# A decoder layer's feed-forward part as seven block products on token halves, and linear attention in 64-column tiles

## The chip, the cores and the metric

One core of a Trainium2 chip runs the whole layer in one launch. The metric is device time in microseconds (us), the median of several runs. In the profile PE is TensorE (PEld its weight loads), DVE is VectorE, ACT is ScalarE, POOL is GpSimd and SP is the queue that issues nearly all DMAs. L200 is line 200 of the kernel.

## The reference

One layer works on 1024 prompt tokens and 8 x 8 sample tokens, 1088 in all, with 1024 features. Everything is float32.

```python
xn = rmsnorm(x, g_mix); proj = xn @ w_in            # linear attention (4 heads) and softmax heads (8)
o_g = rmsnorm(gla(...)) * silu(r)
h = x + concat(o_g, o_s) @ w_out
hn = rmsnorm(h, g_ffn)
y = rmsnorm(h + (silu(hn @ w_fg) * (hn @ w_fu)) @ w_fd, g_final)
```

`w_fg` and `w_fu` are 1024 x 2816, `w_fd` is 2816 x 1024. Linear attention goes in chunks with a state S of 64 x 128 for each head.

## The kernel before

Features lie on the 128 partitions, tokens along the columns, in chunks of 384, 384 and 320 (`CHUNKS`, L32). To keep float32 accuracy at the rate of the `fp32r` type each operand is split in two (`split`, L170): ScalarE rounds it to `hi`, VectorE computes `lo = raw - hi`. A product is then three (`mm3`, L196): hi x hi, hi x lo, lo x hi, added up in PSUM.

The order of the stages: input projection with linear attention in between (`gla_heads`, L537), softmax attention with projections filled in, the first half of the output projection, its second half (L1011 to L1032), feed-forward, final norm.

The second half of the output projection makes the residual `h` for each feature block and chunk and at once `hhi` and `hlo`, the split of `h` times `g_ffn`. The row norm is not in them: `rstd_bc` is multiplied in behind the products.

Feed-forward: there are 22 blocks f of 128 inner features. `ff_up(f)` (L1054) loads and splits the block of the gate and of the up weights, and for each chunk does 8 x 3 products into one PSUM bank for gate and 8 x 3 for up; VectorE multiplies each by `rstd_bc` (L1066, L1068), ScalarE does Silu (L1067), GpSimd gate times up (L1069), and the result is split (L1070). `ff_down` (L1082) takes two blocks at a time and adds 8 x 2 x 3 products for each chunk to `h` (L1090). Every weight is loaded and split once.

The order on each engine comes from the framework's planner, which follows program order, priorities (`tc.high_priority` for weights) and its own idea of durations; each engine then runs its list in that order and waits at the head. DMAs are issued by SP in the same way.

In linear attention each 128-token step (L660) multiplies, for two heads i, the 128-wide `AT` block with the values (L665) and the 128-wide `qE` block with the state (L668), each head into its own bank; copies, squares and the state update follow.

Of the kernel before, what the change touches and what calls it, by code (L numbers as in the profile page):

```python
# [36 lines left out]
BIG = 5  # L37
FILL_AT = (156, 199, 242, 273, 306)
# [64 lines left out]
def hymba_layer(  # L103
# [433 lines left out]
    def gla_heads(g, q, k, V, Vs):  # L537
# [33 lines left out]
        for part in range(3):  # L571
# [86 lines left out]
            if part < 2:  # L658
                otok = gla.tile([P, 8, P], F32, tag="otok", name="otok", bufs=2)
                for c in range(ncmb):  # L660
                    tt = part * 4 + c
                    for i in range(2):
                        o = bank("AX"[i])[:, :P]
                        hs = slice(64 * i, 64 * i + 64)
                        mm(out=o, lhsT=AT[:, i * ncmb + c, :], rhs=V[part][:, c, i * P : (i + 1) * P],  # L665
                           start=True, stop=S is None)
                        if S is not None:
                            mm(out=o, lhsT=qE[hs, c * P : c * P + P], rhs=S[hs, :], start=False, stop=True)  # L668
                        x = 2 * c + i
                        vec.tensor_copy(out=otok[:, x, :], in_=o)  # L670
                        square_sum(o, ssg[:, x : x + 1])
# [331 lines left out]
    late = open_pool("late", side="left")  # L1003
    h = late.tile([P, KT, TT], F32, name="h")
    ff = open_pool("hn", side="right")
    hhi = ff.tile([P, KT, TT], F32R, name="hhi")
    hlo = ff.tile([P, KT, TT], F32R, name="hlo")
    outp = open_pool("outp", side="left")
    ones = outp.tile([P, 1], F32, name="ones")
    vec.memset(ones, 1.0)  # L1010
    os = [load_o(outp, c, 1) for c in range(3)]  # L1011
    sq_acc = [outp.tile([P, 384], F32, tag="acc", name="acc", bufs=3) for _ in CHUNKS]
    for f in range(KT):
        if f % 2 == 0:
            ws = load_w_out(f, 1)
        for c, (c0, n) in enumerate(CHUNKS):
            cs = slice(c0, c0 + n)
            xa = outp.tile([P, 384], F32, tag="xa", name="xa", bufs=4)[:, :n]
            dma(out=xa, in_=x_dram[:, f, cs])
            ps = bank("mm")  # L1020
            mm3(ps[:, :n], ws[f % 2], os[c])
            vec.tensor_tensor(out=h[:, f, cs], in0=ps[:, :n], in1=xa, op=ALU.add)

            act(out=hhi[:, f, cs], in_=h[:, f, cs], func=AF.Copy, scale=gf[:, f : f + 1])
            vec.scalar_tensor_tensor(out=hlo[:, f, cs], in0=h[:, f, cs], scalar=gf[:, f : f + 1],
                                     in1=hhi[:, f, cs].bitcast(F32), op0=ALU.mult, op1=ALU.subtract)
            if f == 0:
                act(out=sq_acc[c][:, :n], in_=h[:, f, cs], func=AF.Square)
            else:
                sq = outp.tile([P, 384], F32, tag="sq", name="sq", bufs=2)  # L1030
                act(out=sq[:, :n], in_=h[:, f, cs], func=AF.Square)
                pool.tensor_tensor(out=sq_acc[c][:, :n], in0=sq_acc[c][:, :n], in1=sq[:, :n], op=ALU.add)  # L1032
    st = outp.tile([P, 3, NTT + 1], F32, name="st")
    vec.memset(st, 1.0)
    tiles = [(c, j, 3 * c + j, min(P, n - j * P)) for c, (_, n) in enumerate(CHUNKS) for j in range(-(-n // P))]
    ps = bank("A")
    for c, j, t, m in tiles:
        mm(out=ps[:m, t : t + 1], lhsT=sq_acc[c][:, j * P : j * P + m], rhs=ones, start=True, stop=True)
    vec.tensor_copy(out=st[:, 0, :NTT], in_=ps[:, :NTT])
    vec.tensor_copy(out=st[:TS, 0, NTT:], in_=ps[:TS, NTT : NTT + 1])  # L1040
    rms(st[:, 1, :], st[:, 0, :], D, st[:, 2, :])
    rows = outp.tile([P, NTT + 1, P], F32, name="rows")
    vec.tensor_copy(out=rows, in_=st[:, 1, :].unsqueeze(2).broadcast_to([P, NTT + 1, P]))
    rb = [bank(tag)[:, :n] for tag, (_, n) in zip("ATT", CHUNKS)]
    for c, j, t, m in tiles:
        nc.tensor.transpose(out=rb[c][:, j * P : j * P + m], in_=rows[:m, t, :], identity=ident[:m, :m])
    for c, (c0, n) in enumerate(CHUNKS):
        vec.tensor_copy(out=rstd_bc[:, c0 : c0 + n], in_=rb[c])
    outp.release()


    ffp = open_pool("ffn", side="left")

    def ff_up(f):  # L1054
        wg_, wu_ = load_w(w_fg[:, f * P : (f + 1) * P]), load_w(w_fu[:, f * P : (f + 1) * P], room=(ffp, "wuraw"))
        ghi = ffp.tile([P, TT], F32R, tag="ghi", name="ghi", bufs=4)
        glo = ffp.tile([P, TT], F32R, tag="glo", name="glo", bufs=4)
        for c0, n in CHUNKS:
            cs = slice(c0, c0 + n)
            xv = ([hhi[:, k, cs] for k in range(KT)], [hlo[:, k, cs] for k in range(KT)])  # L1060
            pg, pu = bank("mm"), bank("S")
# [8 lines left out]
            split(ghi[:, cs], glo[:, cs], gt)  # L1070
        return ghi, glo

    def load_down(f):
        with tc.high_priority():
            raw = wpool.tile([P, D], F32, tag="wraw", name="wd_raw", bufs=1)
            dma(out=raw, in_=w_fd[f * P : (f + 1) * P, :])
# [130 lines left out]
```

## Time and profile before

| what | us |
|---|---|
| median of 3 runs (1580.24 to 1588.89) | 1586.47 |
| the profiled execution | 1588.28 |
| its span in the profile | 1586.4 |
| TensorE busy | 1522.2 |
| VectorE busy | 717.3 |
| ScalarE busy | 435.6 |
| GpSimd busy | 272.1 |

The busy time of TensorE is that of matmuls in flight: they are pipelined, so the rate of products is read from the distance of their starts, not from their lengths. An idle stretch has a releaser, the event that ended it. The granted clock is a share of full speed (1.00 is 2.4 GHz).

### The profile page before, as it was taken

To read this page: it belongs to the slowest core of one execution; us is meant where nothing else is said; L and a number is where in the kernel's file an instruction comes from. 1 tells how busy PE (TensorE), PEld (TensorE's weight loads), DVE (VectorE), ACT (ScalarE), POOL (GpSimd) and SP (SyncE) were. 2 spreads that over 40 slices of the span, in tenths; PEclk is the share of its full clock that TensorE was granted. 3 is DMA by queue.
4 is the path that set the end of the run, shared out by engine and by line. 5 is a ranking of instruction groups with operands and counts; after the bars stand their busy time and mean duration, and the time that the engine had idled before them with its cause. 6 is when DMAs were issued, how large, how long until landed. Compare 5 with 4: busy or idle time off the path is not lost.

```text
span 1586.4 us, 28631 instructions
## 1 busy us (share of the span) xinstructions
PE 1522.2 (96%) x12080; PEld 1377.2 (87%) x12080; DVE 717.3 (45%) x1556; ACT 435.6 (27%) x867; POOL 272.1 (17%) x296
## 2 busy tenths in 40 slices
PE   7979999999999998997999999999999999999997
PEld 6768877887776765767999999999999999999997
DVE  5486575543323233335643443433443343444437
ACT  4143242144342445314421212121111212121113
POOL 1494342042112010002310001010000001010002
PEclk9988999999999999989999999999999999999998
DMA  5320121163443547545321101110211101120102
GB/s 155 92 78 30 30 69 43 41 188 106 136 112 93 153 118 217 177 138 175 92 74 50 54 27 54 41 54 27 67 40 41 54 27 54 40 63 18 54 1 114
DMA packets 177425, 126.73 MB, mean 80 GB/s; under 512 B 14576, under 2 KB 169104, under 8 KB 177296
## 3 DMA queue, kind: packets, MB, share of 16 engines
q1 hardware_dynamic: 173088, 124.69, 26.4%
q8 instruction: 95, 1.56, 0.4%
q10 hardware_dynamic: 4208, 0.21, 0.2%
q14 instruction: 34, 0.28, 0.1%
HBM read 101.40 MB, written 23.46 MB: 79 GB/s over the span
## 4 chain that ended last, share of the span: by engine, by line
PE 86%; DMA 5%; DVE 5%; POOL 1%; issue 1%; ACT 1%; SPq 0%; DVEq 0%; ACTq 0%; POOLq 0%
PE ps_mm L200 13%; PE ps_mm L201 12%; PE ps_mm L202 12%; PE ps_S L202 5%; PE ps_S L201 5%; PE ps_S L200 5%; PE ps_T L201 2%; PE ps_T L200 2%; PE ps_T L202 2%; PE ps_S L835 2%; DMA oraw<-o_dram 2%; PE ps_T L933 2%; PE ps_X L977 2%; PE ps_A L202 1%; PE ps_A L200 1%; PE ps_A L201 1%
## 5 line engine op out<-in xcount | busy, mean ns | idle before, releaser
L200 PE MATMUL ps_mm<-xhi,whi 128*128 128x384 f32 (+1 forms) x576 | 199.5, 347 | 2.0 <-ACT whi L171 1.6
L202 PE MATMUL ps_mm<-xhi,wlo 128*128 128x384 f32 (+1 forms) x576 | 194.6, 339 | 1.1 <-DVE wlo L172 1.1
L201 PE MATMUL ps_mm<-xlo,whi 128*128 128x384 f32 (+1 forms) x576 | 194.8, 339 | 0.2 <-DVE xlo L277 0.2
L1069 POOL TENSOR_TENSOR gt<-gt,ut 128x384 f32<-128x384 f32 (+1 forms) x66 | 64.9, 984 | 698.1 <-DVE ut L1068 698.1
L200 PE MATMUL ps_mm<-hhi,whi 128*128 128x384 f32 (+1 forms) x528 | 172.8, 327 | 1.2 <-DVE gt L1066 1.2
L202 PE MATMUL ps_mm<-hhi,wlo 128*128 128x384 f32 (+1 forms) x528 | 173.0, 328 | 0.0
L201 PE MATMUL ps_mm<-hlo,whi 128*128 128x384 f32 (+1 forms) x528 | 172.8, 327 | 0.0
L200 PE MATMUL ps_S<-hhi,whi 128*128 128x384 f32 (+1 forms) x528 | 172.7, 327 | 0.0
L201 PE MATMUL ps_S<-hlo,whi 128*128 128x384 f32 (+1 forms) x528 | 172.7, 327 | 0.0
L202 PE MATMUL ps_S<-hhi,wlo 128*128 128x384 f32 (+1 forms) x528 | 172.5, 327 | 0.0
L200 PEld LDWEIGHTS ps_mm<-xhi,whi 128*128 128x128 f32 x576 | 110.2, 192 | 13.6 <-issue 7.6
L202 PEld LDWEIGHTS ps_mm<-xhi,wlo 128*128 128x128 f32 x576 | 110.2, 191 | 7.3 <-issue 4.8
L201 PEld LDWEIGHTS ps_mm<-xlo,whi 128*128 128x128 f32 x576 | 110.4, 192 | 5.5 <-issue 4.0
L1067 ACT ACTIVATE gt<-gt 128x384 f32<-128x384 f32 (+1 forms) x66 | 33.1, 502 | 294.6 <-DVE gt L1066 294.6
L1068 DVE TENSOR_TENSOR ut<-ps_S,rstd_bc 128x384 f32<-128x384 f32 (+1 forms) x66 | 35.4, 536 | 159.7 <-PE ps_S L202 159.7
L200 PEld LDWEIGHTS ps_mm<-hhi,whi 128*128 128x128 f32 x528 | 99.2, 188 | 1.4 <-DVE gt L1066 1.4
L201 PEld LDWEIGHTS ps_S<-hlo,whi 128*128 128x128 f32 x528 | 99.2, 188 | 0.0
L202 PEld LDWEIGHTS ps_mm<-hhi,wlo 128*128 128x128 f32 x528 | 99.2, 188 | 0.0
L202 PEld LDWEIGHTS ps_S<-hhi,wlo 128*128 128x128 f32 x528 | 99.2, 188 | 0.0
L200 PEld LDWEIGHTS ps_S<-hhi,whi 128*128 128x128 f32 x528 | 99.2, 188 | 0.0
L201 PEld LDWEIGHTS ps_mm<-hlo,whi 128*128 128x128 f32 x528 | 99.2, 188 | 0.0
L1090 DVE TENSOR_TENSOR h<-h,ps_T 128x384 f32<-128x384 f32 (+1 forms) x120 | 63.5, 529 | 68.1 <-PE ps_T L202 68.1
(335 smaller groups left out, 3048.4 us busy)
## 6 DMA issues: line engine op xcount, KB each, us to landing
wraw<-in_w_in_dram SPq DMA_DIRECT2D x22, 512.0 KB, 3.8
wraw<-in_w_ffn_gate_dram SPq DMA_DIRECT2D x22, 512.0 KB, 3.7
wd_raw<-in_w_ffn_down_dram SPq DMA_DIRECT2D x22, 512.0 KB, 3.2
wuraw<-in_w_ffn_up_dram SPq DMA_DIRECT2D x22, 512.0 KB, 3.7
raw<-in_cache_swa_k_dram SPq DMA_DIRECT2D x32, 256.0 KB, 5.4
raw<-in_cache_swa_v_dram SPq DMA_DIRECT2D x32, 256.0 KB, 4.4
xa<-x_dram SPq DMA_DIRECT2D x32, 192.0 KB, 2.6
xr<-in_x_prompt_dram SPq DMA_DIRECT2D x8, 512.0 KB, 8.4
```

What stands on the lines that cost most here:

```text
L200: mm(out=ps, lhsT=whi[k], rhs=xhi[k], start=first and k == 0, stop=False)
L201: mm(out=ps, lhsT=whi[k], rhs=xlo[k], start=False, stop=False)
L202: mm(out=ps, lhsT=wlo[k], rhs=xhi[k], start=False, stop=last and k == n - 1)
L835: ins = mm(out=out, lhsT=qres[own, qi * P + 32 * r : qi * P + 32 * r + 32], rhs=rhs, start=True, stop=True)
L933: nc.tensor.transpose(out=ps[:, r * P : (r + 1) * P], in_=raw[:, r, :], identity=ident)
L977: mm(out=av[rs, b2 * P : (b2 + 1) * P], lhsT=pT[:, t, rs], rhs=vts[b2][:, r, :], start=False, stop=t == 5 and b2 == 1)
L1067: act(out=gt, in_=gt, func=AF.Silu)
L1068: vec.tensor_tensor(out=ut, in0=pu[:, :n], in1=rstd_bc[:, cs], op=ALU.mult)
L1069: pool.tensor_tensor(out=gt, in0=gt, in1=ut, op=ALU.mult)
L1090: vec.tensor_tensor(out=h[:, k, cs], in0=h[:, k, cs], in1=ps[:, :n], op=ALU.add)
```

## The change

The tokens are cut into two halves of 2 x 272 (`NH = 272`). Weights are seen as 2 x 2 blocks A11, A12, A21, A22 (of output features by input features), activations as B of 2 x 2 (input features by tokens). Instead of eight block products there are seven, M1 to M7, in the Winograd form of Strassen's algorithm: four sums of weight blocks (S1 to S4) and four of activation blocks replace the eighth, and the seven results are combined with more additions.

`winograd` loads four weight blocks, GpSimd makes S1 to S4 in place, each of the seven blocks is split on its own, and every product is 2 x nk x 3 matmuls of 272 columns into a pair of banks. M7, M2, M3 and M4 go on in the bank pair of M6, M1, M5 and M7. `gate_up(i, xs)` does this for two gate and two up blocks (1024 columns a weight block, nk = 4), eleven times for each half of the tokens; `down(i, gs, h)` for two such i at a time (512 columns, nk = 2) in two parts q. So all feed-forward weights are loaded twice. `operand` makes the seven activation operands: four subtractions of 272 columns on GpSimd and splits of 3 x 272 and 4 x 272 columns.

The norm now goes in ahead of the products (`norm_half`), so `hhi` and `hlo` of the old kind are gone. The second half of the output projection is done per half of the tokens (`out_half`, 272 columns); half 1 of the residual goes to DRAM and is read back. The very last feed-forward block of half 1 is multiplied in the ordinary way, in chunks of 224 and 320 columns, with the final norm as before behind the last. In linear attention both products are cut into 64-column halves of the tokens.

```diff
-                    tt = part * 4 + c
+                    halves = (slice(0, 64), slice(64, 128))
+                    os_ = [bank("AX"[i])[:, :P] for i in range(2)]
                     for i in range(2):
-                        o = bank("AX"[i])[:, :P]
-                        hs = slice(64 * i, 64 * i + 64)
-                        mm(out=o, lhsT=AT[:, i * ncmb + c, :], rhs=V[part][:, c, i * P : (i + 1) * P],
-                           start=True, stop=S is None)
-                        if S is not None:
-                            mm(out=o, lhsT=qE[hs, c * P : c * P + P], rhs=S[hs, :], start=False, stop=True)
+                        for ts in halves:
+                            mm(out=os_[i][ts], lhsT=AT[:, i * ncmb + c, ts], rhs=V[part][:, c, i * P : (i + 1) * P],
+                               start=True, stop=S is None)
+                    for ts in halves if S is not None else ():
+                        for i, hs in enumerate(halves):
+                            mm(out=os_[i][ts], lhsT=qE[hs, c * P + ts.start : c * P + ts.stop], rhs=S[hs, :], start=False, stop=True)
+                    for i, o in enumerate(os_):
                         x = 2 * c + i
                         vec.tensor_copy(out=otok[:, x, :], in_=o)
                         square_sum(o, ssg[:, x : x + 1])
...
+    ORDER = (("M1", "A11", 0, "a", True), ("M6", "S2", 4, "b", True), ("M5", "S1", 3, "c", True), ("M7", "S3", 5, "b", False),
+             ("M2", "A12", 1, "a", False), ("M3", "S4", 2, "c", False), ("M4", "A22", 6, "b", False))
+    def blocks(src, w):
...
+        for name, m, k in (("A11", 0, 0), ("A21", 1, 0), ("A22", 1, 1), ("A12", 0, 1)):
+            src(room(name), m, k)
+        add = lambda out, a, b, op: pool.tensor_tensor(out=out, in0=raw[a], in1=raw[b], op=op)
+        add(room("S1"), "A21", "A22", ALU.add)
+        add(raw["A21"], "A11", "A21", ALU.subtract)
+        raw["S3"] = raw["A21"]
+        def parts(name):
+            if name == "S2":
+                add(raw["A11"], "S1", "A11", ALU.subtract)
+                raw["S2"] = raw["A11"]
+            if name == "S4":
+                add(raw["A12"], "A12", "S2", ALU.subtract)
+                raw["S4"] = raw["A12"]
...
+            split(*pair, raw[name])
+            return pair
+        return parts
+    def winograd(src, w, view, x, nk, after):
+        with tc.high_priority():
+            parts = blocks(src, w)
+        banks = {"a": psum2.tile([P, 2, 512], F32, tag="a", name="ps_a", bufs=1)[:, :, :NH]}
+        for name, block, slot, bk, first in ORDER:
+            with tc.high_priority():
+                hi, lo = (view(part) for part in parts(block))
+            if bk not in banks:
+                banks[bk] = psum2.tile([P, 2, 512], F32, tag=bk, name=f"ps_{bk}", bufs=2 if bk == "b" else 1)[:, :, :NH]
+            for s in range(2):
+                for k in range(nk):
+                    xhi, xlo = x(k, slot)
+                    one = lambda l, r, i: mm(out=banks[bk][:, s], lhsT=l[:, k, s], rhs=r, start=first and k == 0 and i == 0,
+                                             stop=k == nk - 1 and i == 2, skip_group_check=not first)
+                    one(hi, xhi, 0)
+                    one(hi, xlo, 1)
+                    one(lo, xhi, 2)
+            after(name, banks)
...
+    def operand(pl, B, tag):
+        t = ffp.tile([P, 4, NH], F32, tag="T", name="T", bufs=1)
+        sub = lambda out, a, b: pool.tensor_tensor(out=out, in0=a, in1=b, op=ALU.subtract)
+        sub(t[:, 0], B[:, 3], B[:, 0])
+        sub(t[:, 2], B[:, 2], B[:, 3])
+        sub(t[:, 1], B[:, 2], t[:, 0])
+        sub(t[:, 3], B[:, 1], t[:, 1])
+        hi, lo = (pl.tile([P, 7, NH], F32R, tag=f"{tag}{part}", name=f"{tag}{part}", bufs=4 if tag == "x" else 3) for part in ("hi", "lo"))
+        split(hi[:, 0:3], lo[:, 0:3], B[:, 0:3])
+        split(hi[:, 3:7], lo[:, 3:7], t)
+        return hi, lo
+    def norm_half(hf):
+        t0 = 2 * NH * hf
+        xs = []
+        for k in range(0, KT, 2):
+            B = new_block()
+            for j, v in ((0, B[:, 0:4:3]), (1, B[:, 1:3])):
+                if hf:
+                    dma(out=v, in_=x_dram[:, k + j, t0 : t0 + 2 * NH].rearrange("p (n t) -> p n t", t=NH))
+                vec.scalar_tensor_tensor(
+                    out=v, in0=v if hf else h[0][:, k + j].rearrange("p (n t) -> p n t", t=NH), scalar=gf[:, k + j : k + j + 1],
+                    in1=rstd_bc[:, t0 : t0 + 2 * NH].rearrange("p (n t) -> p n t", t=NH), op0=ALU.mult, op1=ALU.mult)
+            xs.append(operand(bx, B, "x"))
+        return xs
...
+    def gate_up(i, xs):
+        s1, u2, v5 = temps()
+        B = new_block()
...
+        def made(slot, c, eng):
+            act(out=B[:, slot], in_=c[:, 0], func=AF.Silu)
+            eng.tensor_tensor(out=B[:, slot], in0=B[:, slot], in1=c[:, 1], op=ALU.mult)
...
+        def after(name, ps):
+            add = lambda out, a, b: vec.tensor_tensor(out=out, in0=a, in1=ps[b], op=ALU.add)
+            if name == "M1":
+                act(out=s1, in_=ps["a"], func=AF.Copy)
+            elif name == "M6":
+                add(u2, s1, "b")
+            elif name == "M5":
+                add(v5, s1, "c")
+            elif name == "M7":
+                add(v5, v5, "b")
+                made(2, v5, pool)
+            elif name == "M2":
+                made(0, ps["a"], vec)
+            elif name == "M3":
+                add(u2, u2, "c")
+                made(3, u2, pool)
             else:
+                add(s1, s1, "b")
+                made(1, s1, pool)
+        winograd(src, KT * P, lambda t: t.rearrange("p (s k c) -> p k s c", s=2, c=P),
+                 lambda k, slot: [part[:, slot] for part in xs[k]], KT // 2, after)
+        return B
+    def down(i, gs, h):
+        n = len(gs)
+        hv = h.rearrange("p (q m) (n t) -> p q m n t", m=2, t=NH)
+        for q in range(0, KT // 2, 2):
+            s1, u2, v5 = temps()
...
+            def after(name, ps):
+                to = lambda m, n: hv[:, q : q + 2, m, n]
+                add = lambda out, a, b: vec.tensor_tensor(out=out, in0=a, in1=ps[b], op=ALU.add)
+                more = lambda out, a: pool.tensor_tensor(out=out, in0=out, in1=a, op=ALU.add)
+                if name == "M1":
+                    act(out=s1, in_=ps["a"], func=AF.Copy)
+                    more(to(1, 0), s1)
+                elif name == "M6":
+                    add(u2, s1, "b")
+                    more(to(0, 1), u2)
+                elif name == "M5":
+                    add(v5, s1, "c")
+                    more(to(1, 1), v5)
+                else:
+                    o, bk = {"M7": (to(1, 1), "b"), "M2": (to(0, 0), "a"), "M3": (to(0, 1), "c"), "M4": (to(1, 0), "b")}[name]
+                    add(o, o, bk)
+            winograd(src, n * 2 * P, lambda t: t.rearrange("p (j q c) -> p j q c", q=2, c=P),
+                     lambda k, slot: [part[:, slot] for part in gs[k]], n, after)
+    for hf in range(2):
+        out_half(hf)
+        if hf == 0:
...
+    for hf in range(2):
+        gs = {}
+        for i in range(NF // 2):
+            B = gate_up(i, xs)
+            if hf and i == NF // 2 - 1:
+                break
+            gs[i] = operand(bh, B, "g")
+            if i % 2 == 0 and i >= 2:
+                if hf == 0 and i == NF // 2 - 1:
+                    xs = norm_half(1)
+                down(i - 2, [gs[i - 2], gs[i - 1]], h[hf])
+            if hf and i == 0:
+                for t0 in range(0, 2 * NH, P):
+                    final_rows(0, t0, min(P, 2 * NH - t0))
+                h[1] = residual()
+                dma(out=h[1], in_=x_dram[:, :, 2 * NH :])
+        if hf == 0:
+            down(NF // 2 - 1, [gs[NF // 2 - 1]], h[0])
...
```

## Rows read from the trace of the kernel before

**Rows 1.** the page, part 1: busy us of each engine, share of the span, instructions
```profile
PE 1522.2 (96%) x12080; PEld 1377.2 (87%) x12080; DVE 717.3 (45%) x1556; ACT 435.6 (27%) x867; POOL 272.1 (17%) x296
```

**Rows 2.** the page, part 4: the chain that ended last, by engine
```profile
PE 86%; DMA 5%; DVE 5%; POOL 1%; issue 1%; ACT 1%; SPq 0%; DVEq 0%; ACTq 0%; POOLq 0%
```

**Rows 3.** busy time by stage: stage, length, five engines, clock, DMA share, GB/s
```profile
719.00:782.00 63.00, 55.82 (x327) 55.15 (x325) 36.46 (x61) 32.27 (x61) 23.00 (x21) 0.95 0.40 123
782.00:1560.00 778.00, 776.54 (x4721) 775.68 (x4721) 328.72 (x552) 136.40 (x210) 65.92 (x67) 1.00 0.14 44
1560.00:1587.00 27.00, 16.84 (x103) 15.60 (x101) 19.20 (x54) 10.11 (x25) 9.41 (x10) 0.82 0.43 166
```

**Rows 4.** instructions in time, TensorE, feed-forward: start, length, what (columns 384)
```profile
1008.06 0.33 PE L200 MATMUL ps_X<-ghi,wdhi 128*128 128x384 f32 x1
...
1009.97 0.33 PE L202 MATMUL ps_T<-ghi,wdlo 128*128 128x384 f32 x1
```

**Rows 5.** the same view, input projection, 320 columns
```profile
45.20 0.31 PE L200 MATMUL ps_mm<-xhi,whi 128*128 128x320 f32 x1
...
47.84 0.31 PE L200 MATMUL ps_mm<-xhi,whi 128*128 128x320 f32 x1
```

**Rows 6.** the same view, transposes at the start, four to a row
```profile
41.08 0.60 PE L266 MATMUL ps_T<-ident,xr 128*128 128x128 f32 x4
41.52 0.60 PE L266 MATMUL ps_S<-ident,xr 128*128 128x128 f32 x4
```

**Rows 7.** the same view, GpSimd, sums of 512 and 64 columns
```profile
61.98 2.54 POOL L387 TENSOR_TENSOR xt<-xhi,xlo 128x512 f32<-128x512 f32 x2
...
66.92 0.32 POOL L387 TENSOR_TENSOR xt<-xhi,xlo 128x64 f32<-128x64 f32 x1
```

**Rows 8.** groups by line, VectorE, feed-forward: count, busy us, mean ns, idle before
```profile
L172 DVE TENSOR_TENSOR wlo<-wuraw,whi 128x1024 fp32r<-128x1024 f32 x22 | 33.6, 1526 | 5.0 <-ACT whi L171 5.0
...
L172 DVE TENSOR_TENSOR wlo<-wraw,whi 128x1024 fp32r<-128x1024 f32 x21 | 25.7, 1225 | 12.1 <-ACT whi L171 12.1
L172 DVE TENSOR_TENSOR glo<-gt,ghi 128x384 fp32r<-128x384 f32 x44 | 24.6, 559 | 76.3 <-ACT ghi L171 76.3
L1068 DVE TENSOR_TENSOR ut<-ps_S,rstd_bc 128x384 f32<-128x384 f32 x44 | 24.6, 558 | 129.7 <-PE ps_S L202 129.7
```

**Rows 9.** instructions in time, GpSimd and VectorE, three places where they meet
```profile
828.99 0.88 POOL L1069 TENSOR_TENSOR gt<-gt,ut 128x320 f32<-128x320 f32 x1 [5.96 <-DVE ut L1068]
829.27 1.67 DVE L172 TENSOR_TENSOR wlo<-wuraw,whi 128x1024 fp32r<-128x1024 f32 x1 [0.46 <-ACT whi L171]
...
805.89 1.23 DVE L172 TENSOR_TENSOR wlo<-wuraw,whi 128x1024 fp32r<-128x1024 f32 x1
806.06 1.78 POOL L1069 TENSOR_TENSOR gt<-gt,ut 128x320 f32<-128x320 f32 x1 [1.72 <-DVE ut L1068]
...
854.08 0.88 POOL L1069 TENSOR_TENSOR gt<-gt,ut 128x320 f32<-128x320 f32 x1 [5.97 <-DVE ut L1068]
854.12 0.56 DVE L1090 TENSOR_TENSOR h<-h,ps_A 128x384 f32<-128x384 f32 x1 [0.22 <-PE ps_A L202]
```

**Rows 10.** groups by line, ScalarE, feed-forward
```profile
L171 ACT ACTIVATE whi<-wuraw 128x1024 fp32r<-128x1024 f32 x22 | 23.4, 1063 | 42.0 <-PE ps_S L201 42.0
```

**Rows 11.** the page, part 6: DMA issues, KB each, us to landing
```profile
wraw<-in_w_ffn_gate_dram SPq DMA_DIRECT2D x22, 512.0 KB, 3.7
```

**Rows 12.** instructions in time, TensorE, linear attention
```profile
139.93 0.49 PE L668 MATMUL ps_A<-S,qE 64*128 64x128 f32 x2
140.35 0.49 PE L665 MATMUL ps_X<-V,AT 128*128 128x128 f32 x2
```

**Rows 13.** busy time by stage around the projection's wait (columns as in rows 3)
```profile
724.00:728.00 4.00, 0.00 (x0) 0.00 (x0) 1.36 (x3) 1.03 (x2) 0.00 (x0) 0.91 0.67 237
728.00:732.00 4.00, 2.06 (x7) 2.07 (x8) 1.70 (x4) 1.55 (x4) 0.00 (x0) 0.50 0.02 6
732.00:736.00 4.00, 4.00 (x21) 4.00 (x20) 0.96 (x2) 1.03 (x2) 0.00 (x0) 0.74 0.02 3
```

More of the change, by code (lines that the diff above doesn't have):

```diff
@@ L37 @@
 BIG = 5
+NH = TT // 4
 FILL_AT = (156, 199, 242, 273, 306)
@@ L1033, in hymba_layer @@
[L1033 to L1041, printed above, removed]
@@ new lines, in hymba_layer @@
+    whole = [t.rearrange("p s n -> p (s n)")[:, : 4 * NH].rearrange("p (k n) -> p k n", k=2)
+             for t in (bh.tile([P, 7, NH], F32R, tag=f"g{part}", name=f"g{part}", bufs=3) for part in ("hi", "lo"))]
+    down(NF // 2 - 3, [gs[NF // 2 - 3], gs[NF // 2 - 2]], h[1])
+    wd = []
+    for j in range(2):
+        with tc.high_priority():
+            raw = ffp.tile([P, KT * P], F32, tag="raw", name="raw", bufs=6)
+            dma(out=raw, in_=w_fd[(NF - 2 + j) * P : (NF - 1 + j) * P, :])
+            pair = [wpool.tile([P, KT, P], F32R, tag=part, name=part, bufs=2).rearrange("p k c -> p (k c)") for part in ("whi", "wlo")]
+            split(*pair, raw)
+            wd.append(pair)
@@ new lines, in hymba_layer @@
+    for t, (t0, n) in enumerate(TAIL):
+        c0 = t0 - 2 * NH
+        cs = slice(c0, c0 + n)
+        for k in range(0, KT, 2):
+            ks = [slice(kk * P, kk * P + P) for kk in (k, k + 1)]
+            ps = psum2.tile([P, 2, 512], F32, tag="b", name="ps_d", bufs=2)
+            for j in range(2):
+                mm3(ps[:, j, :n], [[w[part][:, ks[j]] for w in wd] for part in range(2)], [[g[:, i, cs] for i in range(2)] for g in whole])
+            vec.tensor_tensor(out=h[1][:, k : k + 2, cs], in0=h[1][:, k : k + 2, cs], in1=ps[:, :, :n], op=ALU.add)
+            if t:
+                finish(k, c0, n)
+                finish(k + 1, c0, n)
+        rows = [(j * P, min(P, n - j * P)) for j in range(-(-n // P))]
+        if t == 0:
+            for j, m in rows:
+                final_rows(1, t0 + j, m)
@@ new lines, in hymba_layer @@
+    st = fin.tile([P, 12], F32, name="st_last")
+    vec.memset(st, 1.0)
+    sums = psum2.tile([P, 2, 512], F32, tag="b", name="sums", bufs=2)
+    for j in range(3):
+        for part in (acc, last):
+            mm(out=sums[:, 0, j : j + 1], lhsT=part[:, j * P : j * P + P], rhs=one, start=part is acc, stop=part is last)
+    vec.tensor_copy(out=st[:, 0:3], in_=sums[:, 0, 0:3])
+    ps = [psum2.tile([P, 2, 512], F32, tag=tag, name="ps_y", bufs=2 if tag == "b" else 1) for tag in "acb"]
+    for half in range(2):
+        for j, m in rows:
+            for k in range(4):
+                nc.tensor.transpose(out=ps[j // P][:m, half, k * P : k * P + P], in_=h[1][:, 4 * half + k, c0 + j : c0 + j + m], identity=ident)
```

254 lines of the change are left out of this document (121 added, 133 removed).

## The prediction

> **What bounds the kernel now.** I read the page's first part, then the chain that ended last, then busy time by stage, then the feed-forward part instruction by instruction. TensorE is busy 96% of the span, the other three engines 45% and less [rows 1], and 86% of the chain is TensorE [rows 2]. By stage [rows 3]: in 778 us of feed-forward TensorE works 776.5 us at full clock, VectorE 329, ScalarE 136, GpSimd 66; the half of the output projection ahead of it has TensorE busy 56 of 63 us; the tail 17 of 27. So the feed-forward part is matmul time alone, about half of the span. In a run of twelve products of 384 columns the first and last start 1.91 us apart, 11 steps of 0.1736 us [rows 4]; nineteen of 320 columns take 18 steps of 0.1467 us [rows 5]. Before, each chunk costs 22 x 2 x 8 x 3 products for gate and up and 22 x 8 x 3 for down, 1584; two chunks have 384 columns, one 320: 3168 x 0.1736 + 1584 x 0.1467 = 782 us, the stage's length.
>
> **TensorE's new work.** The two rates differ by 0.42 ns a column, so 272 columns should take 0.1467 - 48 x 0.00042 = 0.1265 us. No row shows 272 columns. From above the bound is the 320-column row. From below it is the rate at which 128x128 weights change at all: transposes of 128 columns come four in 0.44 us, 0.11 each [rows 6]. I take 0.1265, since both neighbours lie on one line. A gate-and-up block (call it G) is 7 blocks x 2 x 4 x 3 = 168 products, 21.3 us; half a down step of two feature blocks (D) is 7 x 2 x 2 x 3 = 84, 10.6 us. There are 22 G, 20 D, two half-size d for the odd feature block, and at the end 48 + 48 ordinary products of 224 (0.11) and 320 columns: 5460 x 0.1265 + 48 x 0.11 + 48 x 0.1467 = 703 us, 79 less than before (613 and 813 by the bounds).
>
> The Trainium skill (TensorE: Matmul & The Clock Gate, "Back-to-back issue gap") gives an isolated product N/2.4 + 2.5 ns, an estimate of 116 ns at 272 columns and 58 us less again for the 5460; the sum of TensorE's work would be 645 in place of 703. At 384 and 320 columns the same rule gives 162.5 and 135.8 ns and the rows above are 11 ns slower at both, so I stay on the rows.
>
> **What the other engines get.** GpSimd hardly counted before; now it makes every sum of blocks. Its two-operand operations: two of 512 columns in 2.54 us, one of 64 in 0.32 [rows 7]: 0.18 us + 2.12 ns a column. VectorE's split of 1024 columns takes 1.225 us undisturbed, of 384 columns 0.559 [rows 8]: 0.16 us + 1.04 ns a column.
>
> These two don't add up side by side. GpSimd began 320 columns at 828.99 for 0.88 us; VectorE's split began at 829.27 and took 1.67 instead of 1.225: it ended 1.07 us after GpSimd's end, as if it had waited whole. The other way round, a split from 805.89 to 807.12 made the same GpSimd operation, begun at 806.06, last 1.78: 0.72 after the split's end. But VectorE's add with one operand in PSUM, begun at 854.12 inside a GpSimd operation, took its usual 0.56 [rows 9]. So an operation of VectorE with both inputs in SBUF and one of GpSimd exclude each other (the 22 slow splits in rows 8 show the same mean, 1.526). The time held is 2.12 ns a column + 0.04 for GpSimd, 1.04 + 0.01 for VectorE; the rest of the fixed part can lie beside the other's work. Only the excluding work counts in the next sum.
>
> - G: GpSimd has four sums of 1024 (S1, S3, S2, S4), three multiplications of 272 and four subtractions of 272 for the next operand: 6000 columns, 11 operations, 13.2 us. VectorE has seven splits of 1024 and two for the operand (816, 1088): 9072 columns, 9.5 us. Together 22.7 us against 21.3 of TensorE; with all fixed parts in line 25.6. Between, 24.2.
> - D: four sums of 512 and three adds of 544 into h (`more`) on GpSimd, 3680 columns, 8.1 us; seven splits of 512, 3.8 us: 11.9, in line 13.9, between 12.9, against 10.6. d: 7.8, 9.9, 8.9.
> - `norm_half(1)`: four operands with two scaled copies each, 22.5 us (27.2; 25) beside work that is itself full.
> - The last G needs no operand (-5), the ordinary products at the end 12.3.
>
> Sum: 22 x 24.2 - 5 + 20 x 12.9 + 2 x 8.9 + 25 + 12.3 = 840 us; from below 783, in line 895. I take the middle: hand-overs save fixed parts as rows 9 show, but a pair used to its limit leaves holes. Against 782 that is +58 (bounds +1, +113). The saving of 79 us on TensorE goes into a new bound, the pair VectorE and GpSimd.
>
> The Trainium skill (Advanced Engine Details and Errata, "Mode Summary") says that GpSimd and VectorE block each other in VectorE's two-port modes; a split at 1.04 ns a column is in none, so by that rule it would run free, which is the first rival below. The delayed splits speak against it.
>
> **The chain of weight blocks.** A21 of the next block goes into the buffer of this block's S2 (six `raw` buffers, five used in each block), so its load waits for S4. S4 waits for the split of A12, and that for the buffers of M6's weights (three pairs). Loop from G to G: ScalarE 1.06 [rows 10], VectorE 1.2, S4 2.4, load about 4 [rows 11], S1, S3, S2 7.1, split 2.3, M6 3.0, some 22 us with hand-overs, beside 21.3 of TensorE. D to D comes to 12.8, G to D 14.5, D to G 19.1: 68 us for G, G, D, D, under the 74.2 of the middle sum, but with no room: a load that is late on SP holds A22 and A12 behind it. M7, M2, M3 and M4 also continue in the PSUM of an earlier product and wait for its evacuation, one to two products back. Those adds (0.16 + 544 x 1.04 ns = 0.72 us) stand in VectorE's order behind splits that wait up to 2.4 us for GpSimd, and all of TensorE stands behind the product that waits. I add 8 us for this; below 0, above 60.
>
> Costed at nothing: ScalarE's seven hi copies (7.4 us a G) and four Silu, hidden by TensorE's 21.3 us; if one came late, the split behind it and then a product would wait 1.06 us for it. Twice the weights, about 69 MB in 840 us, is 82 GB/s, below the 123 of the projection stage [rows 3].
>
> **Ahead of it and behind it.** The projection changes 288 products (192 x 0.1736 + 96 x 0.1467 = 47.4 us) to 384 x 0.1265 = 48.6. The first operands need half 0's row statistics (a chain of small VectorE steps) and 25 us of the pair, beside `out_half(1)`'s 24 us of TensorE, where GpSimd has 16 x 0.76 us and VectorE four splits of weights: x is ready later than TensorE. Before, the scaling stood behind the first products. I take +10 (between -8, the idle time in rows 3, and +25). The tail stays as it is (0; 5 either way).
>
> **Linear attention in 64 columns.** A pair of 128-wide products takes 0.42 us start to start where two kinds of tile alternate [rows 12], against 0.22 by rows 6. Four such groups become two in 14 steps: 28 x 0.20 = 5.6 us at most by that count. Halves that run side by side could give 12, twice the instructions cost 8. I take -4.
>
> **The sum.** The profiled execution took 1588.3 us, 1.9 more than its span of 1586.4, and 1.8 over the median of 1586.5. 1586.4 + 58 + 8 + 10 - 4 + 1.9 = 1660 us.
>
> **Rivals.**
> 1. TensorE still bounds: 1586.4 - 79 + 10 - 4 + 1.9 = 1515 us. For: in the feed-forward part it never waited, and each engine alone stays under TensorE's time (GpSimd 14.7 of 21.3 us in G). Against: rows 9. It needs splits and sums to run side by side. 8%.
> 2. The pair is the bound but packs without holes: 783 us, with -4 for the attention and 0 to +10 for the start: 1585 to 1595. For: three weight pairs and six raw buffers decouple. Against: 100% use over 780 us with orders fixed beforehand. 10%, of which 7 within 0.5% and 3 slower.
> 3. Holes in the pair and the chain make TensorE wait in every block, and its clock falls. After 6.7 us without a product the granted clock was 0.50 of full (1.2 GHz) in 728 to 732 and 0.74 in the next 4 us [rows 13], some 3 us lost. With 895 us and such a loss of 2 us in 21 of 42 blocks: +113 + 42 + 6 + 1.9, 1749 us. 22%. It decides once waits of several us stand ahead of M6.
> 4. The forecast, 60%; its own range 1610 to 1710.
>
> Faster by over 0.5% (about what a measurement here can tell from no change) is rival 1, 8%; within it 7%; slower 85%. The range 1590 to 1745 leaves out rival 1, part of rival 2 and the top of rival 3.
>
> **What would show it.** Products of 272 columns 0.1265 us apart; TensorE busy about 85% in the feed-forward part and its waits ended by VectorE's splits; GpSimd's sums of 1024 over 2.4 us and splits over 1.3 us on average; GpSimd and VectorE busy, waits for each other included, nearly all the time. I am wrong if splits keep 1.2 us while GpSimd works, if TensorE is over 95% busy there, or if 272 columns take more than 0.147 us.

## The result and the profile after

Four runs of the changed kernel give 1812.4 us (1801.2 to 1814.8) beside 1587.3 for the kernel before: ratio 1.141, 95% interval 1.136 to 1.147. Slower, as forecast, but by 225 us and not 73; the range ended at 1745. The profiled execution took 1811.2, its span 1809.4.

Busy time, the chain that ended last, and two of the costliest groups (page of the kernel after; busy, mean ns | idle before):

```profile
PE 1545.5 (85%) x13111; PEld 1359.4 (75%) x13111; DVE 1102.8 (61%) x1751; ACT 651.7 (36%) x1143; POOL 894.9 (49%) x657
...
POOL 9%; PE 7%; issue 4%; DVE 4%; ACT 1%; DMA 1%; SPq 0%; POOLq 0%; DVEq 0%; ACTq 0%
...
L1092 POOL TENSOR_TENSOR raw<-raw 128x1024 f32<-128x1024 f32 (+2 forms) x176 | 379.1, 2154 | 320.1 <-DVE wlo L173 165.3
L173 DVE TENSOR_TENSOR wlo<-raw,whi 128x1024 fp32r<-128x1024 f32 (+2 forms) x310 | 422.5, 1383 | 101.0 <-ACT whi L172 96.3
```

No engine is at its limit any more, where TensorE had 96% [rows 1]. The chain, 86% TensorE before [rows 2], is now followed back over a quarter of the span only, and GpSimd leads it. By stage (windows: length, then busy time of PE, PEld, DVE, ACT and POOL, granted clock, DMA share, GB/s): the steady blocks of half 0 (11 gate-and-up blocks, 9 half down steps), the middle between the token halves, the steady blocks of half 1 (9 and 10), and the tail:

```profile
793.00:1232.00 439.00, 367.71 (x2586) 351.52 (x2584) 298.88 (x285) 160.18 (x224) 302.16 (x180) 0.94 0.25 71
1232.00:1369.00 137.00, 92.64 (x570) 87.18 (x571) 101.99 (x156) 46.31 (x70) 82.52 (x57) 0.81 0.33 103
1369.00:1766.00 397.00, 334.20 (x2348) 318.26 (x2347) 282.48 (x268) 146.57 (x210) 281.92 (x172) 0.94 0.25 72
...
1766.00:1809.00 43.00, 25.84 (x152) 22.37 (x151) 23.60 (x61) 8.54 (x17) 5.57 (x6) 0.76 0.15 52
```

The first three, the part by seven products, are 973 us; the whole feed-forward part before was 778, with TensorE busy 776.5 at full clock [rows 3]. Products of 272 columns (timeline of TensorE: start, length) start 0.125 us apart when nothing stops them:

```profile
1460.21 0.28 PE L1131 MATMUL ps_b<-xhi,whi 128*128 128x272 f32 x1
1460.33 0.29 PE L1131 MATMUL ps_b<-xlo,whi 128*128 128x272 f32 x1
1460.46 0.29 PE L1131 MATMUL ps_b<-xhi,wlo 128*128 128x272 f32 x1
1460.58 0.37 PE L1131 MATMUL ps_b<-xhi,whi 128*128 128x272 f32 x1
```

From the starts of all 5460 products: 5460 x 0.1255 = 685 us of work. 179 distances over 0.32 us hold 215 us of waiting. Another 730 or so average 0.225 us and cost 73 us: TensorE at its lower level of 1.2 GHz, most of them in 35 runs of some 16 products, all but the first run behind such waits. One begins behind the four above; the windows view of its middle has the clock at half:

```profile
1461.46:1463.90 2.44, 2.44 (x12) 2.44 (x12) 2.44 (x3) 0.21 (x1) 2.36 (x2) 0.50 0.34 100
```

685 + 215 + 73 is the part's 973. What TensorE waited for there (us in total, times, longest; the largest lines):

```profile
PE ps_b L1131 <- ACT whi L172: 39.7, 20, 8.0
PE ps_b L1131 <- DVE u L1188: 28.6, 12, 4.8
PE ps_c L1131 <- ACT whi L172: 17.0, 18, 4.2
PE ps_c L1131 <- DVE wlo L173: 14.8, 14, 3.5
PE ps_b L1131 <- DVE wlo L173: 13.9, 19, 1.6
...
PE ps_c L1131 <- DVE h L1227: 10.7, 5, 2.9
```

Lines with `whi` and `wlo` are weights that come late, those with `u` and `h` late evacuations (VectorE has not yet read an earlier product out of its bank). Over all lines (idle times above 0.15 us) that is 69 us for `whi`, 41 for `wlo` and 52 for evacuations. Now one gate-and-up block, from M6 to the next block's M6 (timelines of GpSimd, ScalarE, VectorE, TensorE; the bracket is idle time and what ended it):

```profile
1425.16 9.51 POOL L1092 TENSOR_TENSOR raw<-raw 128x1024 f32<-128x1024 f32 x3 [0.63 <-DVE wlo L173]
1442.45 2.41 POOL L1092 TENSOR_TENSOR raw<-raw 128x1024 f32<-128x1024 f32 x1 [7.78 <-DVE wlo L173]
...
1447.68 6.66 POOL L1092 TENSOR_TENSOR raw<-raw 128x1024 f32<-128x1024 f32 x2 [1.42 <-DVE wlo L173]
...
1455.02 2.38 POOL L1092 TENSOR_TENSOR raw<-raw 128x1024 f32<-128x1024 f32 x1
...
1440.00 1.06 ACT L172 ACTIVATE whi<-raw 128x1024 fp32r<-128x1024 f32 x1 [4.24 <-PE ps_b L1131]
...
1441.09 1.23 DVE L173 TENSOR_TENSOR wlo<-raw,whi 128x1024 fp32r<-128x1024 f32 x1 [0.24 <-ACT whi L172]
...
1435.82 0.39 PE L1131 MATMUL ps_b<-xhi,whi 128*128 128x272 f32 x1 [0.34 <-ACT whi L172]
...
1458.54 0.39 PE L1131 MATMUL ps_b<-xhi,whi 128*128 128x272 f32 x1 [2.08 <-ACT whi L172]
```

GpSimd has made S1, S3 and S2 by 1434.7 and then stands 7.8 us: its next item is S4, which overwrites A12, and A12's split waits for the weight buffers of M6, which ends at 1440. Then hi, lo, S4, and for the next block S1, S3 (6.66 us together, 4.7 undisturbed by [rows 7]) and S2; the next M6 starts at 1458.54, 22.7 us after this one. From gate-and-up block to gate-and-up block this is the loop of 22 us of the prediction.

### The profile page after: what moved, and what is told of

It reads as the page before. It is cut to its first block, busy times and chain, and to the rows that moved or that the text cites. A ratio compares the mean times of both kernels' runs of the same rounds, so it can differ in the third digit from the quotient of the medians.

```text
span 1809.4 us, 32741 instructions
## 1 busy us (share of the span) xinstructions
PE 1545.5 (85%) x13111; PEld 1359.4 (75%) x13111; DVE 1102.8 (61%) x1751; ACT 651.7 (36%) x1143; POOL 894.9 (49%) x657
## 5 line engine op out<-in xcount | busy, mean ns | idle before, releaser
L1092 POOL TENSOR_TENSOR raw<-raw 128x1024 f32<-128x1024 f32 (+2 forms) x176 | 379.1, 2154 | 320.1 <-DVE wlo L173 165.3
L173 DVE TENSOR_TENSOR wlo<-raw,whi 128x1024 fp32r<-128x1024 f32 (+2 forms) x310 | 422.5, 1383 | 101.0 <-ACT whi L172 96.3
L172 ACT ACTIVATE whi<-raw 128x1024 fp32r<-128x1024 f32 (+2 forms) x310 | 251.0, 831 | 408.7 <-PE ps_b L1131 191.6
L1131 PE MATMUL ps_b<-xhi,whi 128*128 128x272 f32 x528 | 167.2, 317 | 59.0 <-DVE u L1188 28.6
L1131 PE MATMUL ps_b<-xhi,wlo 128*128 128x272 f32 x528 | 164.3, 311 | 3.9 <-DVE wlo L173 3.9
L1131 PE MATMUL ps_b<-xlo,whi 128*128 128x272 f32 x528 | 162.9, 308 | 0.0
L1131 PEld LDWEIGHTS ps_b<-xhi,whi 128*128 128x128 f32 x528 | 110.6, 209 | 66.8 <-issue 33.5
L1131 PEld LDWEIGHTS ps_b<-xhi,wlo 128*128 128x128 f32 x528 | 110.8, 210 | 5.9 <-DVE wlo L173 5.8
L1131 PEld LDWEIGHTS ps_b<-xlo,whi 128*128 128x128 f32 x528 | 110.8, 210 | 0.0
L1131 PE MATMUL ps_a<-xhi,whi 128*128 128x272 f32 x352 | 104.6, 297 | 5.7 <-ACT whi L172 4.7
```

The costliest lines, as they stand in the source:

```text
L172: a = by.tensor_copy(out=hi, in_=raw) if by else act(out=hi, in_=raw, func=AF.Copy)
L173: return a, vec.tensor_tensor(out=lo, in0=raw, in1=hi.bitcast(F32), op=ALU.subtract)
L1092: add = lambda out, a, b, op: pool.tensor_tensor(out=out, in0=raw[a], in1=raw[b], op=op)
L1131: one = lambda l, r, i: mm(out=banks[bk][:, s], lhsT=l[:, k, s], rhs=r, start=first and k == 0 and i == 0, stop=k == nk - 1 and i == 2, sk ...
```

## Experiments

Times are of one run each, beside 1588 to 1593 us of the kernel before, unless an interval stands with them; theories A to D are defined where they first stand.

**Left out: the sums.**

```diff
-        add(room("S1"), "A21", "A22", ALU.add)          # and S3, S2, S4 alike
+        raw["S1"], raw["S3"], raw["S2"], raw["S4"] = raw["A22"], raw["A21"], raw["A11"], raw["A12"]
```

> Left out: the sums S1 to S4 of weight blocks (the blocks themselves are multiplied in their place, so the result is not the layer's). Theory A (VectorE's splits and GpSimd's sums exclude each other, the pair is the bound) and theory B (the chain of weight buffers S4, A21, S1, S3, S2, split ahead of M6): both lose their ground, TensorE bounds, 1586 - 79 + 12 = 1520 to 1535 us. Theory C (products that go on in a bank wait for a late evacuation, which stands behind splits on VectorE): the waits that adds end stay, 55 us and a third more for the clock: about 1590.

Measured: 1624 us. The three stages of the part by seven products:

```profile
795.00:1143.00 348.00, 332.73 (x2593) 329.27 (x2593) 258.59 (x286) 164.22 (x226) 128.74 (x104) 0.99 0.31 89
1143.00:1265.00 122.00, 91.63 (x574) 85.94 (x575) 92.75 (x156) 45.00 (x69) 44.21 (x38) 0.82 0.38 116
1265.00:1579.00 314.00, 299.21 (x2336) 295.09 (x2335) 241.21 (x268) 148.57 (x210) 116.29 (x93) 0.99 0.31 89
```

439 and 397 us become 348 and 314: of the 214 us by which the steady blocks exceeded their products (4956 x 0.1255 = 622 us), 174 are gone with the sums; gate-and-up blocks run 21.0 us apart without a gap. Splits of 1024 columns are back at 1.24 us. Loads and ScalarE's halves of the splits are as many as in the changed kernel, so neither makes the loss by itself, nor does theory C. The run takes the sums' work and their place in the lists away together and doesn't part theory A from B. All three theories missed the middle: it stays at 122 us, where TensorE's products are 63 (five blocks: 2 x 21.0 + 10.5 + 2 x 5.3).

**Left out: VectorE's half of the weight splits.**

```diff
-            split(*pair, raw[name])
+            act(out=pair[0], in_=raw[name], func=AF.Copy)    # hi alone, used twice
```

> Left out: VectorE's half of every split of feed-forward weights in the seven-block part (hi is multiplied in the place of lo, so the result is not the layer's); all sums stay on GpSimd. Theory A (the splits and the sums hold each other up): GpSimd alone has 14.7 us in a gate-and-up block and 9 in half a down step, TensorE 21.0 and 10.5: TensorE bounds outside the middle, about 1625 as without the sums. Rival (the sums are too slow and stand too late in GpSimd's own list, whatever VectorE does): half of the waits stay, 1700 or more.

Measured: 1650, between the two, nearer to theory A: with the same sums on GpSimd (2.45 us of 1024 columns, 2.77 in the changed kernel) 162 of the 188 us that the sums cost are gone. It takes both engines' work to make the loss. A product also waits for less here, since the lo half is no longer between a sum and its product (1.2 us or more); the run doesn't part that from the amount of work.

**The sums on VectorE.**

```diff
-        add = lambda out, a, b, op: pool.tensor_tensor(...)
+        add = lambda out, a, b, op: vec.tensor_tensor(...)
```

> S1 to S4 on VectorE instead of GpSimd. Theory A: a sum of 1024 costs 1.2 instead of 2.8 us and no longer excludes anything; VectorE has 19.1 us in a gate-and-up block (21.3 of TensorE) and 11.9 in half a down step (10.6): two of each take 66 instead of 86 us, about 1600 in all. Theory B: the chain is 4.8 us shorter, TensorE waits ahead of M6 go, about 1650. Theory C: VectorE has 1.6 times the work ahead of its adds, evacuations come later: 1812 or more.

Measured: 1730, 82 below the changed kernel: the direction of theories A and B, the size of neither. A sum of 1024 columns takes 1.25 us there. Undisturbed gate-and-up blocks again take 21.1 us, but two half down steps 31 us for 21 us of products, VectorE being busy 191 of 225 us (905 to 1130). The Trainium skill (GPSIMD Engine Reference, "Engine selection") gives elementwise work on tiles to VectorE, GpSimd being about twice as slow with two inputs; here it is 1.25 for 2.77 us, both beside other work.

**M2 ahead of M7.**

```diff
-             ... ("M7", "S3", 5, "b", False), ("M2", "A12", 1, "a", False), ...
+             ... ("M2", "A12", 1, "a", False), ("M7", "S3", 5, "b", False), ...
```

> M2 ahead of M7, so that M7 goes on in M6's bank two products later instead of one. Theory C: the 35 us that TensorE waits ahead of M7 in gate-and-up blocks go, with the clock 45: 1765. Theory B: A12 is split and S4 made one product (3 us) earlier, so the next block's A21 too: up to 3 us in each gate-and-up block, 1745. Theory A: the work of the pair is the same, 1812.

Measured: 1773, 39 below the changed kernel; theory A alone, by which nothing changes, misses. The run doesn't part C from B: the waits ahead of M7 in gate-and-up blocks fall from 35 to 20 us (those of them that an evacuation of `u` ended from 29 to 5), but those ahead of M2 rise from 5 to 13; the net gain is ahead of M6, 44 to 23.

**Seven buffers by name, without and with S4 early.**

```diff
-            t = raw[name] = ffp.tile([P, KT * P], F32, tag="raw", name="raw", bufs=6)[:, :w]
+            t = raw[name] = ffp.tile([P, KT * P], F32, tag=name, name="raw", bufs=2 if name in ("A11", "A22") else 1)[:, :w]
# second kernel only:
-            if name == "S4":  add(raw["A12"], "A12", "S2", ALU.subtract)
+            if name == "S1":  add(raw["A11"], "A12", "S2", ALU.subtract)
```

> Seven buffers for weight blocks instead of six, each block name with its own (A11 and A22 two, the others one), so that the next block's A21, S1, S3 and S2 need nothing of this block's S4; the projection's operand buffers are three instead of four for the room. Theory B: the waits ahead of M1, M6 and M5 (115 us in both kinds of block, 150 with the clock) go: about 1680. Theory A: the pair's work is the same, 1800 to 1812. Theory C: 1800 to 1812.

> As the run with seven buffers by name, and S4 is made in the buffer of S2 as soon as S2 is split, three products before the split of A12 that it waited for. Theory D (GpSimd's list of work stops at a sum that overwrites a block whose split itself waits for weight buffers; after it four sums come in one piece and TensorE waits): two gate-and-up blocks and two half down steps take 75 to 79 us, what the pair VectorE and GpSimd needs, instead of 86, so 1715 to 1750 in all. Theory A (the pair is full as it is): 1800 to 1820.

Measured: 1822 and 1756. What GpSimd's sums wait for between 840 and 1740 us, in the changed kernel and then in the first of these runs:

```profile
POOL raw L1092 <- DVE wlo L173: 146.5, 36, 13.6
...
POOL raw L1092 <- DMA raw<-in_w_ffn_up_dram: 94.0, 13, 10.8
...
POOL raw L1092 <- DVE wlo L173: 67.7, 41, 4.0
```

The waits for splits are halved, but the sums now wait for loads, which go out late (one at 1439.45, when a split has ended at 1439.37): A21 and A12 have one buffer each here, so the loop was probably moved and not cut, and the run doesn't settle theory B. With S4 out of that place as well, waits for those loads are 17 us and the kernel is 65 us faster than the first run, 56 faster than the changed kernel. A round (two gate-and-up blocks and two half down steps) takes 81.1 us (1390.5 to 1633.9, three rounds) instead of 85.4 (1427.1 to 1683.4), not quite the 75 to 79 of theory D. In these stretches GpSimd or an instruction of VectorE with two SBUF operands was under way for 73.1 and, in the changed kernel, 72.7 us of each round. The pair's work is the same; what shrinks is the time when neither works, 8.0 instead of 12.7.

**Left out: the final norm of half 0.**

```diff
-                for t0 in range(0, 2 * NH, P):
-                    final_rows(0, t0, min(P, 2 * NH - t0))
```

> Left out: the final norm and the output of half 0, which stands between the first two gate-and-up blocks of half 1. From the changed kernel's trace the second of these blocks takes 42.3 us where its neighbours take 26 to 29, 13.8 of it a wait of TensorE for a bank: 1812 - 15 = 1797 us if only this wait goes; 1785 if the work on ScalarE and VectorE counts as well. By the prediction, which gave it nothing: 1812.

Measured: 1793, 19 less: part of what the middle costs, and nearest to the wait alone (1797).

**Linear attention in 64 columns alone**, on the kernel before.

```diff
-                        mm(out=o, lhsT=AT[:, i * ncmb + c, :], ...)
+                        for ts in halves:  mm(out=os_[i][ts], lhsT=AT[:, i * ncmb + c, ts], ...)   # qE alike
```

> The kernel before with linear attention in 64-column halves and nothing else. The prediction: -4 us (-12 to +8), 1582 beside 1587. Rival: the two products of a pair fill disjoint rows and columns of the array and run side by side, -12: 1575.

Measured: 1582.2, ratio 0.995 (0.993 to 0.997), 8 us; between the prediction's value and the rival's. The rows have halves side by side, as the rival said:

```profile
140.25 0.44 PE L667 MATMUL ps_A<-V,AT 128*64 128x128 f32 x4
140.62 0.44 PE L671 MATMUL ps_A<-S,qE 64*64 64x128 f32 x4
```

Four halves take 0.37 us start to start where two whole products took 0.42 [rows 12], and about half of the halves start 0.01 us or less behind the one before. What part of the array each fills no row shows. Over all these products the distances of the starts sum to 18.5 us instead of 22.3, some 4 us less, the prediction's amount; where the rest of the 8 comes from wasn't followed up.

**All together**, the edits of the order, the seven buffers, S4 early and the sums on VectorE in one kernel:

```diff
-        add = lambda out, a, b, op: pool.tensor_tensor(...)
+        add = lambda out, a, b, op: vec.tensor_tensor(...)    # on top of S4 early; M2 ahead of M7
```

> S4 early, seven buffers by name, M2 ahead of M7, and all four sums on VectorE: all that the runs so far point to. Theory A with D: VectorE has 19.1 us in a gate-and-up block and 11.9 in half a down step, TensorE 21.0 and 10.5: 66 us for two of each, and the middle between the halves keeps its 55 us: 1620 to 1660. If what is left in the vector version (1730) were late evacuations behind VectorE's longer list alone: 1700 or more.

Measured: 1754, 24 above the run with the sums on VectorE alone. The forecast of A with D missed; 1754 lies in the rival's range (1700 or more), but not for the rival's reason: the waits of TensorE that end with evacuations by VectorE fall from 42 to 24 us, those that end with a weight's lo half rise from 30 to 58. These edits don't add up. In half down steps the waits ahead of M1 and M6 fall from 43 to 12 us and those ahead of M7, M3 and M4 rise from 31 to 63, so that their sum stays (83 and 84); in gate-and-up blocks it rises from 63 to 77. Why wasn't followed up.

**Down by ordinary products**, gate and up by seven with sums on VectorE; then also the final norm of half 0 spread.

```diff
-        for q in range(0, KT // 2, 2):                 # down: seven products
+        for q in range(KT // 2):                       # one block of 4 x 256 columns, split once
+            for s in range(2): for m in range(2):  mm3(ps[:, m], ...)   # 4 feature blocks x 3 products
# second kernel:
-                for t0 in range(0, 2 * NH, P):
-                    final_rows(0, t0, min(P, 2 * NH - t0))
-                h[1] = residual()
+            if hf and i < 5:
+                final_rows(0, i * P, min(P, 2 * NH - i * P))
+                h[1] = bh.tile([P, KT, 2 * NH], F32, name="h1")    # at i == 0
```

> Gate and up by seven blocks with the sums on VectorE, down by ordinary products on the same token halves (24.1 us of TensorE for four feature blocks in place of 21.0; no sums, four activation operands to split instead of seven). If, as the vector version's trace shows, gate-and-up blocks run at 21.1 us and the waits come with the down steps: 797 + 22 x 21.0 + 253 + 43 + 2 = 1557, with some 40 us in the middle between the halves 1600. If the waits come with any block whose weights are summed: 1650 or more.

> The same, with the final norm of half 0 spread over five gate-and-up blocks and a second buffer for the residual, instead of all five row tiles in one place. From the run that left this norm out (-19 us) and the 14 us for which a product waited there for a bank: 15 to 20 us below the version before, 1580.

Measured: 1587.7, ratio 0.9997 (0.998 to 1.002), within what was expected with the middle's cost, and 1563.7, ratio 0.985 (0.982 to 0.988): 24 us below the first for 15 to 20 expected, and 1.5% below the kernel before. The windows of the second, and all waits of TensorE over 0.15 us in the first window:

```profile
790.00:1530.00 740.00, 731.36 (x5821) 729.21 (x5821) 562.26 (x643) 285.08 (x354) 105.01 (x85) 1.00 0.33 100
1530.00:1562.00 32.00, 16.96 (x84) 14.49 (x84) 16.86 (x46) 6.16 (x13) 5.70 (x6) 0.67 0.20 71
...
PE ps_A L1068 <- DVE rows L1065: 6.0, 1, 6.0
PE ps_d L201 <- DVE h L1239: 1.7, 2, 1.3
PE ps_b L1134 <- DVE u L1191: 0.9, 1, 0.9
PE ps_c L1134 <- DVE u L1191: 0.8, 1, 0.8
```

TensorE is busy 731 of 740 us and bounds again, at full clock. Seven products for eight pay where the other engines have room for them.

**The sums back on GpSimd in this version, without and with S4 early.**

```diff
-        add = lambda out, a, b, op: vec.tensor_tensor(...)
+        add = lambda out, a, b, op: pool.tensor_tensor(...)
```

> The spread hybrid (1564 us) with the four sums back on GpSimd. A gate-and-up block then has four sums of 1024 and three multiplications of 272 on GpSimd (10.7 us held) and splits of 7 x 1024 and 1088 columns on VectorE (8.7): 19.4 us against 21.0 of TensorE, and four down columns far less. If only the amount of the pair's work counts: 1564 to 1580. If the holes count (S4 waits for the split of A12, then S1, S3 and S2 follow in one piece, 19 us from M6's end to the next M6): 3 to 5 us lost in each of 22 blocks, 1630 to 1670.

> The same with S4 made in S2's buffer as soon as S2 is split. If the holes count and S4's wait is their cause: half or more of the loss of the run before comes back, 1580 to 1610. If the amount counts: as the run before within 10 us.

Measured: 1593 and 1589. The first is 13 above the range of "the amount" and 37 below that of the holes; the second gives back 4 of the 29 us lost, as "the amount" said. Sums (2.74 us) are as slow as in the changed kernel and splits (1.49) nearly, and GpSimd waits longer for splits, yet TensorE is busy 741.6 of 770 us:

```profile
790.00:1560.00 770.00, 741.56 (x5821) 732.94 (x5821) 515.36 (x557) 283.63 (x354) 330.54 (x169) 0.99 0.31 96
...
L1092 POOL TENSOR_TENSOR raw<-raw 128x1024 f32<-128x1024 f32 x85 | 233.1, 2743 | 288.4 <-DVE wlo L173 211.1 <-issue 66.9 <-DVE st L156 8.2
```

So holes cost little while the pair has less work (19.4 us) than TensorE (21.0), and much where it has more.

**The exclusion by itself**, additions of 512 columns behind the kernel before.

```diff
+    for i in range(6):  two(pool, m[3], m[0], m[2] if i == 0 else m[3])     # GpSimd, three times alike
+    for i in range(8):  two(vec, m[4], m[0], m[2] if i == 0 else m[4])      # beside it: two SBUF operands
+    for i in range(12): vec.tensor_tensor(out=m[7], in0=m[7], in1=bk, op=ALU.add)     # bk in PSUM
+    for i in range(12): vec.tensor_scalar(out=m[10], in0=m[10], scalar1=1.0, ...)
```

> The kernel before with a measurement behind it: additions of 512 columns, six on GpSimd alone, six on VectorE alone, then both side by side with VectorE's two operands in SBUF, then with one in PSUM, then with one operand only (a scaling). Theory A: alone 1.27 and 0.69 us; side by side with two SBUF operands the times add, about 2.0 for a pair; with a PSUM operand 1.27 and 0.69 as if alone. Rival (they share a path and each only slows down): GpSimd's get longer by a fifth in all three.

Measured (timeline: start, length of the run of instructions, their number), GpSimd's rows first, then VectorE's: alone, side by side with two SBUF operands on VectorE, with one of two in PSUM, with one operand; the last row is the same scaling when GpSimd has ended:

```profile
1588.34 6.62 POOL L1182 TENSOR_TENSOR m<-m,m 128x512 f32<-128x512 f32 x5
1599.46 10.04 POOL L1182 TENSOR_TENSOR m<-m,m 128x512 f32<-128x512 f32 x6 [4.50 <-DVE m L1182]
1611.65 7.99 POOL L1182 TENSOR_TENSOR m<-m,m 128x512 f32<-128x512 f32 x6 [2.15 <-DVE m L1191]
1621.16 8.43 POOL L1182 TENSOR_TENSOR m<-m,m 128x512 f32<-128x512 f32 x6 [1.53 <-DVE m L1196]
...
1594.99 4.33 DVE L1182 TENSOR_TENSOR m<-m,m 128x512 f32<-128x512 f32 x6 [5.82 <-POOL m L1182]
...
1600.08 9.97 DVE L1182 TENSOR_TENSOR m<-m,m 128x512 f32<-128x512 f32 x6
...
1611.60 8.62 DVE L1182 TENSOR_TENSOR m<-m,ps_A 128x512 f32<-128x512 f32 x12
...
1621.51 8.37 DVE L1200 TENSOR_SCALAR m<-m 128x512 f32<-128x512 f32 x6
...
1629.91 2.27 DVE L1200 TENSOR_SCALAR m<-m 128x512 f32<-128x512 f32 x5
```

Start to start an addition takes 1.34 us on GpSimd and 0.73 on VectorE alone. With two SBUF operands both step by 1.67 us, one addition of each in turn: more than either alone, less than the 2.07 of both in line (2.0 expected). The held parts of the prediction give just that, 1.13 + 0.54 = 1.67: they exclude each other, the fixed parts overlap. With a PSUM operand nothing changes, 1.34 and 0.72. With one SBUF operand a scaling, 0.46 alone, takes 1.40 and GpSimd's addition 1.40, again one of each in turn. The rival, a slowdown of GpSimd by a fifth in all three, falls. The Trainium skill (VectorE: DVE Perf Modes, "Two Vector instructions with no wait between them") says that an instruction with two SBUF tensor inputs reads its second one through an interface shared with GpSimd; the first stretch side by side agrees. The Trainium skill (Advanced Engine Details and Errata, "Mode Summary") says that GpSimd and VectorE block each other in VectorE's two-port modes; the last stretch would agree if a scaling runs in such a mode, which no row here names.

## Why the prediction was right and wrong

**Right.** TensorE's work: 0.1255 us for 272 columns (0.1265 forecast), 685 us (691). The Trainium skill (TensorE: Matmul & The Clock Gate, "Back-to-back issue gap") gives an isolated product of this size an estimated 0.116 us; the rows here don't reach it. The new bound, too: VectorE and GpSimd exclude each other as forecast, with sums at 2.77 and splits at 1.71 us (over 2.4 and 1.3 forecast), while adds with a PSUM operand keep their 0.72. And the amount of the pair's work in a round: 2 x 24.2 + 2 x 12.9 = 74.2 us forecast, 72.7 measured.

**Wrong: the step "I take the middle" of the pair's sum, with "68 us ... under the 74.2" and 8 us for late evacuations.** It took the pair's work for the time. Pair and TensorE wait for each other in the same loop, with three pairs of weight buffers between them, and neither is ever full: TensorE's products need 63 us of a round and its lower clock adds to that, the pair needs 73, the round takes 85.4. The pair is at work in 85% of it, where the prediction named "nearly all the time" as a sign. The chain was wrongly left out because it was shorter than the pair's sum: its waits don't lie beside the pair's work, they are the pair's holes, and where S4 no longer waits the round is 4.3 us shorter with the same work. The chain was also right in part only. Over the steady rounds M6 follows M6 after 24.3 us from G to G and 19.5 from D to G (22 and 19.1 in the prediction), but after 24.0 from G to D and 18.6 from D to D (14.5 and 12.8); from G to D TensorE's own products between the two already take 19.6. How much of the 12.7 us of holes comes from S4 and how much from the other waits isn't separated beyond that. Outside the middle that is 439 + 397 = 836 us against 20 x 24.2 + 19 x 12.9 = 729 and the 8: about 99 us of the 151 that the span (1809.4 against 1658.4) missed. Late evacuations are part of it: they ended 52 us of TensorE's waits, not 8.

**Wrong: the middle.** D, two d, two G and `norm_half(1)` were 104 us; they took 137. The final norm of half 0, priced at nothing, is 19 of the 33 by the run without it: five row tiles go one after the other through two banks, and M6 of the next block needs one of them. Where the other 14 go stays open.

**Small terms.** The feed-forward part begins at 793.6, not at 788, although linear attention gave 8 instead of 4: the start costs 19 and not 10. The end is 43.2 us instead of 38.7 (26.4 and the ordinary products' 12.3). The last 9 of the 151 are the -5 for the block without an operand, and the 4 us by which the stage before (778) was shorter than its products' sum (782), both in the forecast and not in the 729.

**The rivals.** Rivals 1 and 2 are out: what the rows showed to exclude each other does not run side by side, and the pair does not pack. Rival 3 is what happened, holes in pair and chain and a falling clock, with 1812 for its 1749. Its point of decision was right too: waits ahead of M6 are the largest, 44 us in gate-and-up blocks and 27 in half down steps (there with 28 ahead of M3). Its clock loss was 42 us, measured 73; its sum of fixed parts (+113) stood for the holes, which are larger. It should have been the forecast: with the chain at 68 and the pair at 74 us of a round, both close to each other and in one loop, the sum should have been nearer to the upper bound than to the middle.

**Open.** With S4 early the pair still stands idle 8.0 us of 81.1. Which of the remaining orders (S3 ahead of S2, adds behind splits, three weight pairs) keeps it so wasn't separated; there was no room for a fourth weight pair.

## What to carry to other kernels

When a change trades products for sums, add up per block what each other engine gets, count instructions that exclude each other as one engine, and go ahead only if that sum stays clearly below TensorE's block: at 19.4 for 21.0 us a block lost 1.3 us ((1593 - 1564) / 22), at 73 for 63 the holes added more than the excess itself (12.7 and 10). A sum written over a block that must first be split puts the split's wait at the head of an in-order list; give it another place (worth 56 us here, 4 where the pair had room). Do the part whose sums fit (here gate and up) and leave the other as it was.

## What was not expected of the hardware

VectorE's scaling with one SBUF operand excludes GpSimd's additions too, and the shorter instruction pays: it takes 1.40 us instead of 0.46, GpSimd's addition 1.40 instead of 1.34 (5% more). An estimate by the prediction's held parts fits: of the scaling's 0.43 us 0.15 are its fixed part, and 0.28 + 1.13 = 1.41. And the lower clock is a second price of short waits: behind waits of 2.1 and 0.4 us sixteen products ran at the half clock; 215 us of waiting brought 73 us of such products with it.
